# Four modulation vectors moved into attention and onto VectorE, a fourth projection bank, and S5 operators on VectorE

## Chip, cores, metric

The kernel runs on one core of one Trainium2 chip. The metric is the device time of one execution in microseconds (us). Three executions of the kernel before took 2083.79, 2084.78 and 2093.15 us, so the median is 2084.78. The profile and the trace come from a fourth execution, which took 2093.97 us.

## What is computed

Two blocks, one after the other, on 512 tokens of width 1024, in fp32. The first block is a modulated mixer (a bidirectional state-space scan called SSD, windowed attention with 256 context keys, gates and an output projection) and a convolutional feed-forward layer. The second block joins forgetting attention, a diagonal complex state-space layer (S5) and attention to a memory. Of all this the change touches two things.

The modulation is six vectors of 1024, made from one conditioning vector:

```python
mod = jax.nn.silu(c) @ w_mod[l] + b_mod[l]
sh1, sc1, gt1, sh2, sc2, gt2 = jnp.split(mod[:, None, :], N_MOD, axis=-1)
```

Numbered 0 to 5. Vectors 0 and 1 scale and shift the mixer's input and are needed at once. Vector 2 gates the mixer's output, 3 and 4 shift and scale the feed-forward layer's input, 5 gates its output.

The S5 layer needs operators that depend on weights alone: per group of 16 channels, maps into and out of the state over blocks of eight tokens, and powers of the state's rotation over 64 blocks. They are computed on the chip, ahead of the second block.

## The kernel before

All work is in one function, `emit`, written against a tile library. The program names tiles from pools with a number of buffers; the library gives each engine its order. A planner does so when the program is built: it runs through the program in a simulation of the engines and lets each engine take, of the instructions that are ready in the simulation, the one that was written first (`high_priority` moves instructions forward, `issue_after` holds them behind another instruction of the same engine). On the chip each engine then works through its own order, and waits where an operand or a buffer isn't ready.

**Weights.** `load_w` loads 512 KB of fp32 weights into a tile `raw` (three buffers, on SP's DMA queue), copies it on ScalarE into `whi` (rounded to fp32r), and subtracts on VectorE for the low half `wlo`; both have two buffers. `dense` runs three matmuls for each of 8 blocks of 128 rows: high by high (L221), high by low (L222), low by high (L223). A full block of weights is 24 matmuls of 512 columns. The outputs are PSUM banks from `bank()`, tag "d": three of them, two during attention (`set_banks`).

**Stages in order** (us of the profiled span). Until 46: norms and modulation vectors 1 and 0. From 46 to 577, the SSD stage: for each of 16 tiles `ssd_in` projects x, B, C and z, `convs` reads the projection's bank with ScalarE and VectorE, and `ssd_heads` does the scan; `ssd_out` projects every fourth round. From 577 to 631 keys and values; from 631 to 858 attention, eight pairs of heads (`att_q`, `att`), with gates (`gate_ssd`) and, from the fifth pair on, the first half of the output projection (`half_proj` into `p2`) between. From 858 to 990 the rest of the mixer's output. From 990 to 1405 the feed-forward layer: `ffn_up(0)`, `ffn_down(0)`, `ffn_up(1)`, `ffn_down(1)`. Then the second block.

**Modulation vectors.** `mod_steps` makes one vector in eight steps. Each step has a `raw` tile with 128 rows of the vector's 1024 columns and runs four matmuls over 256 columns each, with 32 columns of weights (`csil`, whose first two columns hold the silu of the conditioning); they add up in one PSUM bank, in its four groups of 32 partitions. After the last step ScalarE copies the bank, two transposes bring it into column form, and VectorE adds the bias into `modx`. Vectors 2 and 3 run with the SSD stage, two steps a round from round 5 on, in a bank of their own (`psm`, tag "m"); vector 4 runs in attention from the fifth pair on, in one of the two "d" banks; vector 5 runs in `ffn_up(0)` in a pool of two banks (`pfb`).

**S5 operators.** `s5_operators` is a generator, one piece of which is let go at fixed places of the feed-forward loops (`S5_UP`, `S5_DOWN`). Its preparation works on VectorE. Then come six rounds q: `op_maps(q)` builds `bm` and `cm` from six tensor-tensor operations of 1024 and 1152 elements per partition, on GpSimd, with scratch `x_`; `op_mm(q)` transposes and multiplies them on TensorE (its output tile uses the slot of `x_` too) and stores the results; `op_rot(q)` builds the rotations by six doublings, three operations each, on 16 to 512 elements, on GpSimd. The stores go out on GpSimd's queue (`QS`). They are read in the second block, from 1440 us on.

Of the kernel before, what the change touches and what calls it, by code (L numbers as in the profile page):

```python
# [8 lines left out]
F32 = mybir.dt.float32  # L9
# [5 lines left out]
PSUM = bass.MemoryType.PSUM  # L15
DRAM = bass.MemoryType.DRAM

P = 128
# [138 lines left out]
def emit(ctx, tc, A, out):  # L157
    nc = tc.nc

    def pool(name, bufs=1, **kw):  # L160
        return tc.tile_pool(name=name, bufs=bufs, reuse_waits="tile", **kw) if "space" not in kw else \
            tc.tile_pool(name=name, bufs=bufs, **kw)
# [46 lines left out]
    def bank(name="d"):  # L209
        return banks["p"].tile([P, 512], F32, tag="d", name=name, bufs=banks["n"])  # L210
# [122 lines left out]
            tt(modc[:, r, :].rearrange("p (j b) -> p b j", b=2), v[:, :, :, 1], bm, ADD)  # L333
        yield

    def mod_raw(r):
        def src(k):
            raw = wp.tile([P, 1024], F32, tag="raw", name="raw", bufs=3)
            DMA.dma_start(out=raw, in_=A["w_mod"][k * P:(k + 1) * P, r * 1024:(r + 1) * 1024])
            return raw  # L340
        return src

    def run(steps):
        for _ in steps:
# [98 lines left out]

    pss = ExitStack()
    ro = pss.enter_context(pool("rowsout"))
    ps = pss.enter_context(tc.tile_pool(name="pss", bufs=1, space=PSUM, reuse_waits="tile"))

    def pst(name="t"):
# [240 lines left out]
    def psm(name):  # L689
        return ps.tile([P, 512], F32, tag="m", name=name, bufs=1)  # L690

    mods = [st_ for r in (2, 3) for st_ in [mod_steps(r, mod_raw(r), 1, psm)] * 8]
    with tc.issue_after(loaded.ins), tc.issue_after(mod_end[0]):
        ssd_in(0)
    hold.clear()
# [1 line left out]
    for kt in range(16):  # L697
        if kt < 14:
            ssd_in(kt + 1)
        ssd_heads(kt)  # L700
        if kt >= 5 and kt < 13:
            for _ in range(2):
                next(mods.pop(0))
        if kt % 4 == 1 and kt > 1:
            if kt == 13:
                ssd_in(15)
            ssd_out(kt // 4 - 1)
# [193 lines left out]
    DMA.dma_start(out=s5ls, in_=A["s5p"][:, 96:144])  # L901
    att_q(0)
    first = half_proj(A["w_oa"][0], yaa, lambda m, po: act(p2[:, m], po, AF.Copy))
    mod4 = mod_steps(4, mod_raw(4))
    fill = {1: [0], 2: [1], 3: [2], 4: [3], 5: [4], 6: [5, 6], 7: [7]}
    for i in range(8):
        if i < 7:
            att_q(i + 1)
        done = att(i)
        if i == 1:  # L910
            with tc.issue_after(done.ins):
                act(s5ls, s5ls, AF.Exp)
        for m in fill.get(i, []):
            gate_ssd(m)
        if i >= 4:
            next(first)
            next(mod4)
    stt(g2, modx[:, 4, :], 1.0, col("n2g", 0, 8), ADD, MUL)
    psa.close()

# [91 lines left out]
    def s5_operators(so, pso):  # L1012
# [131 lines left out]
        def op_maps(q):  # L1144
            gs_ = slice(8 * q, 8 * q + 8)
            bc_ = so.tile([P, 4, P], F32, tag="bc_", name="bc_")
            DMA.dma_start(out=bc_, in_=A["s5p"][:, 144:].rearrange("p (a n) -> p a n", a=4)[:, :, P * q:P * q + P])

            def w4(n, k):
                return bc_[:, n].rearrange("p (g c) -> p g c", g=8).unsqueeze(2).to_broadcast([P, 8, k, 16])  # L1150
            bm = so.tile([P, 8, 8, 16], F32, tag="bm", name="bm")
            cm = so.tile([P, 8, 9, 16], F32, tag="cm", name="cm")
            x_ = so.tile([P, 8, 9, 16], F32, tag="x_", name="x_")
            tt(bm, w4(0, 8), tb1[:, gs_, ::-1].unsqueeze(3).to_broadcast([P, 8, 8, 16]), MUL, eng=G)
            tt(x_[:, :, 0:8], w4(1, 8), tb2[:, gs_, ::-1].unsqueeze(3).to_broadcast([P, 8, 8, 16]), MUL, eng=G)
            tt(bm, bm, x_[:, :, 0:8], ADD, eng=G)
            x_ = so.tile([P, 8, 9, 16], F32, tag="x_", name="x_")
            tt(cm, w4(2, 9), tc1[:, gs_].unsqueeze(3).to_broadcast([P, 8, 9, 16]), MUL, eng=G)
            tt(x_, w4(3, 9), tc2[:, gs_].unsqueeze(3).to_broadcast([P, 8, 9, 16]), MUL, eng=G)
            tt(cm, cm, x_, ADD, eng=G)  # L1160
            maps[q] = (bm, cm)
            return QS.dma_start(out=s5c2[q], in_=cm)

# [25 lines left out]
        def op_rot(q):  # L1189

            gs_ = slice(8 * q, 8 * q + 8)
            e3 = so.tile([P, 3, 8, 64], F32, tag="e3", name="e3o")
            G.memset(e3[:, 0, :, 0:1], 1.0)
            G.memset(e3[:, 1, :, 0:1], 0.0)
            x_ = so.tile([P, 2, 8, 32], F32, tag="xe", name="xe")
            for m in range(6):
                w = 1 << m
                new, xx = e3[:, 0:2, :, w:2 * w], x_[:, :, :, 0:w]
                tt(new, e3[:, 0:2, :, 0:w],
                   ec_[:, gs_, m:m + 1].unsqueeze(1).to_broadcast([P, 2, 8, w]), MUL, eng=G)  # L1200
                tt(xx, e3[:, 1::-1, :, 0:w],
                   esx[:, :, gs_, m:m + 1].to_broadcast([P, 2, 8, w]), MUL, eng=G)
                tt(new, new, xx, ADD, eng=G)
            G.tensor_copy(e3[:, 2], mg[:, gs_, 8:9].to_broadcast([P, 8, 64]))
            G.memset(e3[:, 2, :, 0:1], 0.0)
            QS.dma_start(out=s5e[:, :, gs_], in_=e3)

# [33 lines left out]
    pme.close()  # L1241
    so = ExitStack()
    spool = so.enter_context(pool("s5o", side="right"))
    pf_s = ExitStack()
    pf = pf_s.enter_context(tc.tile_pool(name="pffn", bufs=1, space=PSUM, reuse_waits="tile"))

    def pfb(name):
        return pf.tile([P, 512], F32, tag="f", name=name, bufs=2)

    mod5 = mod_steps(5, mod_raw(5), 1, pfb)  # L1250
    actf = (lambda k: hf[:, 0, k], lambda k: hf[:, 1, k])

    def conv_raw(pa, t, o):
# [8 lines left out]
        with tc.issue_after(last[0].ins), tc.issue_after(last[1].ins), tc.issue_after(ld.ins):  # L1262
            next(s5_steps, None)

    MOD_UP = (0, 1, 2, 3, 4, 5, 6, 7)
    S5_UP = (1, 2, 3, 4, 5, 6, 7, 8, 9, 12, 14, 15, 17)
    S5_DOWN = (0, 1, 4, 5, 7)

    def ffn_up(half):
        ph, pl2 = [], []  # L1270
        for j in range(11):
            t = 11 * half + j
            pa = bank("ua")
            with tc.issue_after(after[0].ins):
                dense(flat(A["w_up"][t]), KD, [actf], [pa])
            sa = ft("sa")
            conv_raw(pa, t, sa)
            act(sa, sa, AF.Silu)
            pb = bank("ub")
            dense(flat(A["w_up"][22 + t]), KD, [actf], [pb])  # L1280
            vb = ft("vb")
            conv_raw(pb, 22 + t, vb)
            tt(vb, vb, sa, MUL)
            uh = fd.tile([P, L], F32R, tag="uh", name="uh", bufs=14)
            ul = fd.tile([P, L], F32R, tag="ul", name="ul", bufs=14)
            split(uh, ul, vb)
            ph.append(uh)
            pl2.append(ul)
            if t in MOD_UP:
                next(mod5)  # L1290
            if t in S5_UP:
                s5_next()
        return (lambda k: ph[k], lambda k: pl2[k])
# [28 lines left out]
                tt(a_, a_, sq, ADD)  # L1322
    run(s5_steps)
    ps5_s.close()
    pf_s.close()
    so.close()


# [501 lines left out]
```

## Time and profile before

| | |
|---|---|
| median of three executions | 2084.78 us |
| the profiled execution | 2093.97 us |
| its span in the trace | 2092.2 us |
| mean granted clock of TensorE | 0.982 of full speed |

How to read the rows below. PE is TensorE's matmuls, PEld its weight loads, DVE VectorE, ACT ScalarE, POOL GpSimd, SP the engine that issues most loads. L221 is a line of the kernel; lines 181, 184 and 187 are helpers for an activation, a tensor-tensor and a scalar-tensor-tensor operation, so there the tile's name tells what is done. A matmul's duration holds its way through the array: matmuls overlap, and the distance of two starts is what one costs.

A row of busy time by stretch has the stretch, its length, for PE, PEld, DVE, ACT and POOL busy us with the number of instructions, then TensorE's mean granted clock, the DMA engines' share and GB/s. A row of waits names the waiting instruction, what released it, the total us, how often, and the longest. A row of a group has line, engine, operation, output<-inputs, shapes and count, then busy us, the mean ns of one, and the idle time before. A row of the timeline has start, duration, engine, line, operation and count. A row of DMA issues ends with the count, KB each, and us from issue to landing.

### The profile page before, as it was taken

How to read it: one execution, taken by the hardware profiler on the slowest of the kernel's cores; microseconds unless marked ns; L12 is line 12 of the kernel's file. 1: busy time of each engine (PE TensorE's matmuls, PEld its weight loads, DVE VectorE, ACT ScalarE, POOL GpSimd, SP SyncE). 2: the span in 40 equal slices, each digit the busy share in tenths (PEclk: the TensorE clock that was granted, in tenths of full speed). 3: DMA queues.
4: the chain of work that ended last, by engine and by line, in shares of the span. 5: the costliest groups of instructions: out<-in, count | busy, mean ns of one | idle time of the engine just before them, and what ended most of it. 6: DMA issues, size and time to landing. Idle time of an engine off the chain costs nothing.

```text
span 2092.2 us, 29510 instructions
## 1 busy us (share of the span) xinstructions
PE 1986.9 (95%) x11312; PEld 1623.7 (78%) x11312; DVE 1350.6 (65%) x2195; ACT 964.1 (46%) x1825; POOL 416.6 (20%) x539
## 2 busy tenths in 40 slices
PE   6998999998999999999999899999999899999998
PEld 4777887787788777778777677787988777888887
DVE  6878978878547775457975477664677655524444
ACT  6745555454235665334433133445465544423233
POOL 2123321212130000001054787200333100000000
PEclk9999999999999999999999999999999999999999
DMA  7443545544322023343343444436565221332332
GB/s 289 121 132 121 154 143 162 163 142 135 98 71 71 21 73 90 106 129 95 121 152 99 133 131 154 131 116 183 157 170 149 54 66 56 126 104 91 101 91 91
DMA packets 84668, 250.49 MB, mean 120 GB/s; under 512 B 11632, under 2 KB 23280, under 8 KB 83760
## 3 DMA queue, kind: packets, MB, share of 16 engines
q1 hardware_dynamic: 67376, 199.45, 30.9%
q0 software_dynamic: 17152, 49.17, 7.7%
q8 instruction: 89, 1.46, 0.3%
q14 instruction: 51, 0.42, 0.1%
HBM read 228.78 MB, written 16.65 MB: 117 GB/s over the span
## 4 chain that ended last, share of the span: by engine, by line
PE 76%; DVE 11%; issue 6%; ACT 4%; DMA 2%; POOL 1%; SPq 0%; DVEq 0%; ACTq 0%; POOLq 0%
PE p L221 6%; PE p L223 6%; PE p L222 6%; PE pl L221 4%; PE pl L223 4%; PE pl L222 4%; DVE wlo L184 3%; PE pT L807 2%; PE po L221 2%; PE pdn L223 2%; PE po L222 2%; PE po L223 2%; PE pdn L221 2%; PE ua L223 2%; PE pdn L222 2%
## 5 line engine op out<-in xcount | busy, mean ns | idle before, releaser
L184 DVE TENSOR_TENSOR wlo<-raw,whi 128x1024 fp32r<-128x1024 f32 (+3 forms) x283 | 367.3, 1299 | 341.4 <-ACT whi L181 329.5
L181 ACT ACTIVATE whi<-raw 128x1024 fp32r<-128x1024 f32 (+3 forms) x283 | 282.4, 999 | 445.0 <-PE p L222 138.4
L221 PE MATMUL pl<-hl,whi 128*128 128x512 f32 x528 | 211.7, 401 | 5.6 <-DVE cv L187 3.8
L223 PE MATMUL pl<-hl,wlo 128*128 128x512 f32 x528 | 209.7, 397 | 0.9 <-DVE wlo L184 0.7
L222 PE MATMUL pl<-hl,whi 128*128 128x512 f32 x528 | 209.8, 397 | 0.0
L223 PE MATMUL p<-h,wlo 128*128 128x512 f32 x504 | 202.0, 402 | 1.1 <-DVE wlo L184 1.1
L221 PE MATMUL p<-h,whi 128*128 128x512 f32 x504 | 201.1, 401 | 1.9 <-ACT uf L181 0.8
L222 PE MATMUL p<-h,whi 128*128 128x512 f32 x504 | 201.7, 400 | 0.0
L221 PEld LDWEIGHTS pl<-hl,whi 128*128 128x128 f32 x528 | 100.4, 190 | 25.1 <-issue 4.4
L223 PEld LDWEIGHTS pl<-hl,wlo 128*128 128x128 f32 x528 | 100.3, 190 | 22.9 <-DVE wlo L184 2.5
L221 PEld LDWEIGHTS p<-h,whi 128*128 128x128 f32 x504 | 95.5, 189 | 25.0 <-ACT uf L181 1.2
L181 ACT ACTIVATE p<-s,nm 128x512 f32<-128x512 f32 (+4 forms) x128 | 80.2, 627 | 74.4 <-PE pT L807 35.2
L223 PEld LDWEIGHTS p<-h,wlo 128*128 128x128 f32 x504 | 95.3, 189 | 23.2 <-DVE wlo L184 2.0
L782 DVE TENSOR_REDUCE nm<-s 128x1 f32<-128x512 f32 (+4 forms) x128 | 76.6, 611 | 55.7 <-PE s L1592 30.1
L222 PEld LDWEIGHTS p<-h,whi 128*128 128x128 f32 x504 | 95.3, 189 | 22.0 <-DVE h L184 0.3
L222 PEld LDWEIGHTS pl<-hl,whi 128*128 128x128 f32 x528 | 100.4, 190 | 15.2
L181 ACT ACTIVATE inj<-cs_t,dwt 128x128 f32<-128x128 f32 x256 | 81.4, 393 | 63.3 <-DVE es L635 56.0
L181 ACT ACTIVATE pt<-pT 128x512 f32<-128x512 f32 (+1 forms) x152 | 70.7, 479 | 63.1 <-PE pT L807 52.5
L640 POOL DMA_DIRECT2D cf<-rows x64 | 34.9, 552 | 298.2 <-PE y L659 292.8
L807 PE MATMUL pT<-cs_t,p 128*128 128x128 f32 x440 | 72.8, 279 | 9.9 <-ACT pt L181 9.6
L223 PE MATMUL pdn<-uh,wlo 128*128 128x512 f32 x176 | 70.9, 403 | 8.8 <-DVE wlo L184 8.8
L223 PE MATMUL ua<-hf,wlo 128*128 128x512 f32 x176 | 70.8, 402 | 8.8 <-DVE wlo L184 8.8
(543 smaller groups left out, 4955.1 us busy)
## 6 DMA issues: line engine op xcount, KB each, us to landing
raw<-in_w_ta SPq DMA_DIRECT2D x66, 512.0 KB, 3.6
raw<-in_w_tb SPq DMA_DIRECT2D x63, 512.0 KB, 3.6
raw<-in_w_up SPq DMA_DIRECT2D x44, 512.0 KB, 3.7
es<-rows POOLq DMA_DIRECT2D x64, 256.0 KB, 5.2
cf<-rows POOLq DMA_DIRECT2D x64, 256.0 KB, 4.9
raw<-in_w_mod SPq DMA_DIRECT2D x32, 512.0 KB, 3.8
raw<-in_w_os SPq DMA_DIRECT2D x16, 512.0 KB, 3.6
raw<-in_w_out SPq DMA_DIRECT2D x16, 512.0 KB, 3.8
```

Source lines behind the costliest of these rows:

```text
L181: return S.activation(o, i, f, **kw)
L184: return eng.tensor_tensor(o, a, b, op=op)
L221: T.matmul(ps, lhsT=wh, rhs=ah, start=first, stop=False)
L222: T.matmul(ps, lhsT=wh, rhs=al, start=False, stop=False)
L223: T.matmul(ps, lhsT=wl, rhs=ah, start=False, stop=last)
L640: QS.dma_start(out=c_, in_=rows[r, 1].partition_broadcast(P))
L782: V.tensor_reduce(nm[:, j:j + 1], src, axis=AX.X, op=MAX)
L807: T.transpose(pt[:, j * P:(j + 1) * P], b, ident)
```

## The change

Vectors 2 to 5 are no longer made by matmuls over 256 columns. A new `mod_sums` loads the same 32 `raw` tiles, and VectorE adds each, times its 128 conditioning values, to a scratch `acc` (the part of `p2` for tiles 6 and 7). After eight such steps TensorE sums over the partitions: eight matmuls with 128 columns of `acc` as weights and one column of ones, into a "t" bank of attention's pool; VectorE adds the bias. All 32 steps stand in attention, five behind each of the first four pairs of heads, four behind each of the next three.

The PSUM bank of tag "m" in the SSD stage goes, and the "d" banks there become four. The pool of two banks in the feed-forward stage goes too.

In `op_maps` and `op_rot` the tensor-tensor operations and the copy go from GpSimd to VectorE; the small memsets and the stores stay.

```diff
-    def mod_raw(r):
-        def src(k):
+    def mod_sums(r, step, bank, acc):
+        for k in range(KD):
             raw = wp.tile([P, 1024], F32, tag="raw", name="raw", bufs=3)
             DMA.dma_start(out=raw, in_=A["w_mod"][k * P:(k + 1) * P, r * 1024:(r + 1) * 1024])
-            return raw
-        return src
+            ck = csil[:, k, 0:1]
+            if k == 0:
+                V.tensor_scalar(acc, raw, ck, None, op0=MUL)
+            else:
+                stt(acc, raw, ck, acc, MUL, ADD)
+            if k % step == step - 1 and k < KD - 1:
+                yield
+        ps = bank("mod")
+        for j in range(8):
+            T.matmul(ps[:, j:j + 1], lhsT=acc[:, j * P:(j + 1) * P], rhs=ones[:, 0:1], start=True, stop=True)
+        tt(modx[:, r, :], ps[:, 0:8], col("bmod", r * 8, 8), ADD)
+        yield
...
     ro = pss.enter_context(pool("rowsout"))
+    set_banks(4)
...
-    mods = [st_ for r in (2, 3) for st_ in [mod_steps(r, mod_raw(r), 1, psm)] * 8]
...
-        if kt >= 5 and kt < 13:
-            for _ in range(2):
-                next(mods.pop(0))
...
-    mod4 = mod_steps(4, mod_raw(4))
+    mods = [st_ for r in (2, 3, 4, 5) for st_ in [mod_sums(r, 1, pst, p2[:, 6:8].rearrange("p k t -> p (k t)"))] * 8]
...
         if i >= 4:
             next(first)
-            next(mod4)
+        for _ in range((5, 5, 5, 5, 4, 4, 4, 0)[i]):
+            next(mods.pop(0))
...
-            tt(bm, w4(0, 8), tb1[:, gs_, ::-1].unsqueeze(3).to_broadcast([P, 8, 8, 16]), MUL, eng=G)
+            tt(bm, w4(0, 8), tb1[:, gs_, ::-1].unsqueeze(3).to_broadcast([P, 8, 8, 16]), MUL)
...
-            tt(cm, cm, x_, ADD, eng=G)
+            tt(cm, cm, x_, ADD)
...
-                tt(new, new, xx, ADD, eng=G)
-            G.tensor_copy(e3[:, 2], mg[:, gs_, 8:9].to_broadcast([P, 8, 64]))
+                tt(new, new, xx, ADD)
+            V.tensor_copy(e3[:, 2], mg[:, gs_, 8:9].to_broadcast([P, 8, 64]))
...
-    mod5 = mod_steps(5, mod_raw(5), 1, pfb)
...
-            if t in MOD_UP:
-                next(mod5)
```

The lines left out repeat the same step for the other operations of `op_maps` and `op_rot`, or take away the pool of two banks and the constant `MOD_UP`.

## Rows read from the trace of the kernel before

**Rows 1.** Part 1 of the page: busy time, share of the span, instructions.

```profile
PE 1986.9 (95%) x11312; PEld 1623.7 (78%) x11312; DVE 1350.6 (65%) x2195; ACT 964.1 (46%) x1825; POOL 416.6 (20%) x539
```

**Rows 2.** Busy time of each engine in five stretches of the span.

```profile
46.00:577.00 531.00, 501.41 (x3234) 421.64 (x3234) 421.72 (x671) 259.53 (x565) 117.35 (x162) 0.96 0.44 138
631.00:858.00 227.00, 216.48 (x1667) 173.91 (x1666) 151.01 (x332) 141.80 (x321) 7.69 (x6) 1.00 0.21 63
990.00:1124.00 134.00, 132.03 (x608) 99.21 (x608) 106.89 (x198) 57.25 (x81) 35.14 (x35) 1.00 0.40 125
1124.00:1348.00 224.00, 205.55 (x941) 163.62 (x941) 143.80 (x117) 72.21 (x101) 150.10 (x183) 0.95 0.43 134
996.00:1048.00 52.00, 51.05 (x235) 36.77 (x234) 48.16 (x129) 24.49 (x33) 0.12 (x1) 1.00 0.40 123
```

**Rows 3.** Waits of PE in the SSD stage, 46 to 577 us.

```profile
PE pc L221 <- DVE cv L187: 9.0, 2, 4.5
PE po L221 <- DVE cvc L187: 4.5, 2, 3.3
PE pl L221 <- DVE cv L187: 3.8, 1, 3.8
...
PE pc L221 <- ACT zs L181: 2.6, 1, 2.6
```

**Rows 4.** Groups of DVE instructions in the feed-forward stage, 990 to 1348 us.

```profile
L184 DVE TENSOR_TENSOR wlo<-raw,whi 128x1024 fp32r<-128x1024 f32 x51 | 91.6, 1796 | 83.1 <-ACT whi L181 79.1 <-PE o L1171 3.7
...
L184 DVE TENSOR_TENSOR ul<-vb,uh 128x512 fp32r<-128x512 f32 x22 | 29.7, 1348 | 12.6 <-ACT uh L181 12.6
...
L184 DVE TENSOR_TENSOR sm<-sm,sm 128x432 f32<-128x432 f32 x9 | 5.4, 604 | 0.0
...
L184 DVE TENSOR_TENSOR sm<-sm,sm 128x48 f32<-128x48 f32 x22 | 4.4, 208 | 0.2
```

**Rows 5.** Timeline of DVE around the longest stall, 1163 to 1181 us.

```profile
1163.08 8.58 DVE L184 TENSOR_TENSOR wlo<-raw,whi 128x1024 fp32r<-128x1024 f32 x1 [4.03 <-ACT whi L181]
...
1179.64 1.23 DVE L184 TENSOR_TENSOR wlo<-raw,whi 128x1024 fp32r<-128x1024 f32 x1 [3.84 <-ACT whi L181]
```

**Rows 6.** Timeline of POOL there: first and last of seven instructions.

```profile
1163.10 0.74 POOL L184 TENSOR_TENSOR e3o<-e3o,xe 128x256 f32<-128x256 f32 x1
...
1170.54 2.24 POOL L184 TENSOR_TENSOR e3o<-e3o,xe 128x512 f32<-128x512 f32 x1
```

**Rows 7.** Timeline of PE around one step of a modulation vector.

```profile
1088.74 0.39 PE L222 MATMUL ub<-hf,whi 128*128 128x512 f32 x1
1088.96 0.39 PE L223 MATMUL ub<-hf,wlo 128*128 128x512 f32 x1
1089.28 0.63 PE L320 MATMUL mod<-raw,csil 128*32 128x256 f32 x4
1089.84 0.50 PE L221 MATMUL ua<-hf,whi 128*128 128x512 f32 x1
```

**Rows 8.** DMA issues of the page: loads of w_mod one step long.

```profile
raw<-in_w_mod SPq DMA_DIRECT2D x32, 512.0 KB, 3.8
```

**Rows 9.** Timeline of PE where eight one-column matmuls stand.

```profile
1409.05 1.84 PE L262 MATMUL cs<-cs_t,a 128*128 128x1 f32 x16
1410.75 0.47 PE L221 MATMUL pv<-whi,hm 128*128 128x512 f32 x1
```

**Rows 10.** Groups of DVE instructions in attention, 631 to 858 us.

```profile
L797 DVE TENSOR_SCALAR p<-p,sm 128x640 f32<-128x640 f32 x32 | 17.5, 548 | 0.0
```

**Rows 11.** The chain behind the longest stall (start, us, what); six like the second follow.

```profile
1171.71 0.79 PE pdn L223
1172.51 0.43 PE pdn L221
```

**Rows 12.** Waits of POOL, 990 to 1348 us.

```profile
POOL x__10286 L184 <- DMA s5w<-w1o: 4.8, 1, 4.8
POOL x__11390 L184 <- DMA s5w<-w1o: 4.2, 1, 4.2
```

More of the change, by code (lines that the diff above doesn't have):

```diff
@@ L1153, in op_maps @@
             x_ = so.tile([P, 8, 9, 16], F32, tag="x_", name="x_")
-            tt(bm, w4(0, 8), tb1[:, gs_, ::-1].unsqueeze(3).to_broadcast([P, 8, 8, 16]), MUL, eng=G)
-            tt(x_[:, :, 0:8], w4(1, 8), tb2[:, gs_, ::-1].unsqueeze(3).to_broadcast([P, 8, 8, 16]), MUL, eng=G)
-            tt(bm, bm, x_[:, :, 0:8], ADD, eng=G)
+            tt(bm, w4(0, 8), tb1[:, gs_, ::-1].unsqueeze(3).to_broadcast([P, 8, 8, 16]), MUL)
+            tt(x_[:, :, 0:8], w4(1, 8), tb2[:, gs_, ::-1].unsqueeze(3).to_broadcast([P, 8, 8, 16]), MUL)
+            tt(bm, bm, x_[:, :, 0:8], ADD)
             x_ = so.tile([P, 8, 9, 16], F32, tag="x_", name="x_")
-            tt(cm, w4(2, 9), tc1[:, gs_].unsqueeze(3).to_broadcast([P, 8, 9, 16]), MUL, eng=G)
-            tt(x_, w4(3, 9), tc2[:, gs_].unsqueeze(3).to_broadcast([P, 8, 9, 16]), MUL, eng=G)
-            tt(cm, cm, x_, ADD, eng=G)
+            tt(cm, w4(2, 9), tc1[:, gs_].unsqueeze(3).to_broadcast([P, 8, 9, 16]), MUL)
+            tt(x_, w4(3, 9), tc2[:, gs_].unsqueeze(3).to_broadcast([P, 8, 9, 16]), MUL)
+            tt(cm, cm, x_, ADD)
             maps[q] = (bm, cm)
@@ L1199, in op_rot @@
                 tt(new, e3[:, 0:2, :, 0:w],
-                   ec_[:, gs_, m:m + 1].unsqueeze(1).to_broadcast([P, 2, 8, w]), MUL, eng=G)
+                   ec_[:, gs_, m:m + 1].unsqueeze(1).to_broadcast([P, 2, 8, w]), MUL)
                 tt(xx, e3[:, 1::-1, :, 0:w],
-                   esx[:, :, gs_, m:m + 1].to_broadcast([P, 2, 8, w]), MUL, eng=G)
-                tt(new, new, xx, ADD, eng=G)
-            G.tensor_copy(e3[:, 2], mg[:, gs_, 8:9].to_broadcast([P, 8, 64]))
+                   esx[:, :, gs_, m:m + 1].to_broadcast([P, 2, 8, w]), MUL)
+                tt(new, new, xx, ADD)
+            V.tensor_copy(e3[:, 2], mg[:, gs_, 8:9].to_broadcast([P, 8, 64]))
             G.memset(e3[:, 2, :, 0:1], 0.0)
@@ L1243, in emit @@
     spool = so.enter_context(pool("s5o", side="right"))
[L1244 to L1248, printed above, removed]
-    mod5 = mod_steps(5, mod_raw(5), 1, pfb)
     actf = (lambda k: hf[:, 0, k], lambda k: hf[:, 1, k])
@@ L1263, in s5_next @@
             next(s5_steps, None)
-    MOD_UP = (0, 1, 2, 3, 4, 5, 6, 7)
     S5_UP = (1, 2, 3, 4, 5, 6, 7, 8, 9, 12, 14, 15, 17)
@@ L1324, in emit @@
     ps5_s.close()
-    pf_s.close()
     so.close()
```

## The prediction

> **What bounds the kernel now.** First the page's part 1 [rows 1]: TensorE's matmuls cover 95% of the span, VectorE 65%, ScalarE 46%, GpSimd 20%. So whatever leaves TensorE's queue shortens the kernel, as long as nothing else is late where it leaves. Then busy time by stage [rows 2]. In the SSD stage (46 to 577 us) TensorE idles 531 - 501.4 = 29.6 us, in attention (631 to 858) 10.5, in the first part of the feed-forward stage 2.0 and in its second part (1124 to 1348) 224 - 205.55 = 18.45, there with a mean granted clock of 0.95. Two of these have one kind of cause. In the SSD stage the waits of a projection's first matmul are for the convolution or the silu that still reads a projection bank [rows 3]: these four make 19.9 us. In the second part of the feed-forward stage the wait is for the low half of the weights (wlo) on VectorE, and that subtraction is itself stretched: 51 of them take 1.796 us in the mean [rows 4], against 1.23 us where GpSimd rests, the last of [rows 5]. The worst lasts 8.58 us [rows 5], and through it GpSimd runs S5 work, seven instructions one after the other from 1163.10 to 1172.78 [rows 6].
>
> **The vectors' matmuls go.** One step of a modulation vector on TensorE stands between the matmuls at 1088.96 and 1089.84 [rows 7]: 0.88 us where the spacing is otherwise 0.22 (1088.74 to 1088.96), so it costs 0.66. There are 32 steps, one per load [rows 8]: 21.1 us, 10.6 in the SSD stage, 5.3 in attention, 5.3 in the feed-forward stage. The transposes and the copy behind each vector are left out. In their place come four times eight matmuls of one column with 128 weight columns. The same form stands at 1409.05, sixteen records for eight matmuls, and the next matmul begins 1.70 us later [rows 9]: 4 x 1.7 = 6.8 us, all in attention. Net -14.3 us; attention's TensorE work grows by 1.5. The Trainium skill (TensorE: Matmul & The Clock Gate, "Wait — 56ns, not 53.3ns?") gives a start-to-start floor of about 25 ns however few the columns; by that the 64 records would cost an estimated 1.6 us and the forecast would fall by 5. The row has 0.106 us per record, the weight loads included, so the row is taken.
>
> **The vectors on VectorE, in attention.** 28 multiply-adds over 128x1024 have two SBUF inputs as wlo has: 28 x 1.23 = 34.4 us. The four that begin a vector have one tensor; a tensor-scalar of 640 takes 0.548 us [rows 10], so between that and 1.23, say 0.9: 3.6 us. Together 38 us. Attention's VectorE load goes from 151 to 189 of 227 us [rows 2], 67% to 83%. The queue is in order: behind each multiply-add stand the softmax's maxima and scalings and the next wlo; each waits for its load, 3.8 us from issue to landing [rows 8], and for the sum before it. On SP's queue 24 more 512 KB loads come into this stage, and a weight load behind one waits for the same three raw slots; so far such slots were held until TensorE came to the step, now VectorE frees them. Bounds: nothing, if all 38 us fall into the 76 us in which VectorE rests, up to 38, if each holds up the softmax and through it TensorE. TensorE's idle time there is 10.5 us at 67%; I take half of that again, +5, since the rows are nearer to hidden than to exposed. The sums' scratch is the part of p2 that the half projection's last pair of tiles fills, so a late last vector would hold one of the two projection banks; that is in the upper bound. The bank that the fifth vector held through the second half of attention comes free; its gain is taken as nothing.
>
> **The fourth bank in the SSD stage.** The trace has no run with four. Bounds: nothing, if the convolutions simply stay late (VectorE is busy 421.7 of 531 us there), and the 19.9 us of [rows 3]. A bank more lets one further projection (24 x 0.22 = 5.3 us) run before the oldest bank must be drained, longer than the longest of these waits, 4.5. But VectorE at 79% will set the next wait. I take half, -10.
>
> **The S5 maps and rotations move.** On VectorE a tensor-tensor costs 0.158 us + 1.03 ns per element, from 48 and 432 elements [rows 4]. Six rounds of three operations on 1024 and three on 1152: 18 x 1.21 + 18 x 1.35 = 46 us. Six rounds of 18 rotations of 16 to 512 elements (3024 in all): 6 x (18 x 0.158 + 3.1) = 36; six copies of at most 0.69: 4. Together 86 us. Against that the stretching goes: wlo 51 x (1.796 - 1.23) = 29, ul 22 x (1.348 - 0.69) = 14.5 [rows 4]. VectorE then has 250.7 + 86 - 43 = 293 us of work in stages that shrink from 358 to about 330: 89%. What TensorE gets back: the 18.45 us of idle time, and the half speed behind it. After the 8.58 us stall the matmuls go at 0.43 us to 1175.49 [rows 11], the 1.2 GHz level, against 0.22; about 2 us each for the three such stalls, 6 in all. So up to -24.5. What is late next: VectorE itself. Three map operations that do not depend on each other (3.8 us) can stand ahead of a wlo that has some 3 us to spare (5.3 less 1.23 and the like on ScalarE): 0.8 x 5. And the maps' scratch slot waits for a DMA, 4.8 and 4.2 us [rows 12]; on GpSimd nobody stood behind, on VectorE a wlo does: 9.0 less twice 3 makes 3. I take +7, bounds 0 and the rival below. The S5 stores and small memsets stay on GpSimd's queue, where they wait for VectorE instead; only the second half of the kernel reads them. Net -17.5.
>
> **Sum.** -14.3 + 5 - 10 - 17.5 = -36.8 us. The profiled execution took 2093.97 us, 9.2 above the median of the runs shown, 2084.78; taken from the median, 2048.
>
> **Rivals.** (a) Attention becomes VectorE's: the multiply-adds hold up the softmax at their full length. For it: 83% load, an in-order queue, waits for loads inside it. Against it: 38 us of rest remain, and each blocks for 1.23 us only. Then +38 instead of +5: 2081, no change. (b) Slower: the planner puts a whole S5 round (6 map operations and 19 others, 86 / 6 = 14.3 us) in front of a wlo in the feed-forward stage, in the five rounds that wait for an earlier round's matmuls and so come late. TensorE then idles 14.3 - 3 = 11.3 and gets 2 us of half speed, 13.3 x 5 = 66 instead of 7: +59, so 2107. It decides from (36.8 + 7) / 5 = 8.8 us per round on. Against it: from 996 to 1048 VectorE already runs S5's preparation between the wlo, busy 48.16 of 52 us, and TensorE loses one, the last of [rows 2]. The Trainium skill (Perfetto Trace Analysis, "Optimizing Scalar/DVE Operations") says that with VectorE saturated, moving work to GpSimd may make sense; that speaks for this rival, and [rows 4, 5] against it as long as the two collide. (c) The change does not do what it says: the fourth bank leaves the waits where they are, and VectorE's own S5 work takes all that the collisions cost. Left is -14.3 + 5: 2075.
>
> **Numbers.** A difference of 0.5%, 10.4 us, is about what a measurement of this kernel can tell from none. Forecast (all terms about as sized, or better) 0.68; (a) 0.12; (b) 0.10; (c) 0.10, on the border, half to either side. Faster 0.73, same 0.17, slower 0.10. Low end: all four bank waits gone, no new waits on VectorE: -14.3 - 19.9 - 24.5 = -58.7, and the 2 us of the first feed-forward part and some half speed in the SSD stage, 2020. High end: (a) with some waits beside it, 2086; above it lies (b).
>
> **What would show it.** Right: no one-step modulation matmuls in the SSD and feed-forward stages; wlo near 1.23 us throughout the feed-forward stage and TensorE's idle time there under 10 us; the waits of [rows 3] halved; VectorE at some 190 us in attention with TensorE idling 15. Wrong: wlo short but late, behind S5 operations; TensorE idle for more than 25 us in attention; the convolution waits unchanged.

## The result and the profile after

The kernel after took 2063.38 us (median of four, 2062.18 to 2066.59), the kernel before 2084.28 (four, three of them those known before the prediction, 2080.72 to 2093.15). The ratio is 0.9894, 95% interval 0.9866 to 0.9922: faster by 20.9 us, where 36.8 were forecast. The profiled execution of after took 2063.76 us; it lies 30.2 us below the one of before, which was the longest of the first executions of that kernel. In 39 executions run later beside the experiments, on three chips, the kernel before took 2081.17 to 2098.54 us, with a median of 2091.83; so the four executions of this comparison lie on its short side, and 20.9 us may be too little. The kernel after wasn't run again there. Later comparisons are therefore made as ratios to runs of the kernel before on the same chip, and the stages below from the profiled executions.

Part 1 of the page, answering [rows 1]:

```profile
PE 1964.2 (95%) x11112; PEld 1622.0 (79%) x11112; DVE 1395.9 (68%) x2377; ACT 962.2 (47%) x1821; POOL 263.8 (13%) x389
```

TensorE is busy for 22.7 us less, VectorE for 45 more, GpSimd for 153 less. Busy time by stage (stretch, length, then PE, PEld, DVE, ACT and POOL busy with counts, granted clock, DMA share, GB/s), answering [rows 2]:

```profile
46.00:559.10 513.10, 483.07 (x3092) 410.62 (x3091) 418.27 (x667) 257.84 (x562) 119.25 (x163) 0.98 0.42 125
614.00:858.00 244.00, 228.01 (x1666) 186.42 (x1664) 181.24 (x365) 140.90 (x321) 9.55 (x7) 0.97 0.32 100
989.70:1116.90 127.20, 124.29 (x562) 100.55 (x562) 117.58 (x247) 59.25 (x85) 9.53 (x18) 1.00 0.36 111
1116.90:1372.80 255.90, 252.73 (x1177) 204.14 (x1176) 182.00 (x280) 100.53 (x146) 20.89 (x49) 0.99 0.43 134
```

Cut where work ends on TensorE, the first block has three stages. **A** goes from 46 us to the last matmul on `yh`, the SSD stage's output projection: 528.8 us before, 513.1 after. **B** goes from there to the first matmul on `mgh`, so it holds keys and values, attention, and the second half of the output projection: 348.4 before, 365.1 after. **C** goes from there to the last matmul of `pdn`, so it is above all the feed-forward layer: 480.0 before, 448.6 after. So A gives 15.7 us, C gives 31.4, and B takes 16.7 back. The second block is as long as before.

**A.** TensorE's waits from 46 to 559.1 us, answering [rows 3] (waiting instruction, releaser, us, times, longest):

```profile
PE pl L221 <- DVE cvc L187: 8.1, 2, 6.9
PE pl L221 <- ACT p L181: 5.1, 1, 5.1
PE po L221 <- ACT yh L181: 3.5, 1, 3.5
PE pl L221 <- ACT zs L181: 1.7, 1, 1.7
...
PE pc L221 <- DVE cv L187: 0.9, 1, 0.9
```

The two waits of 9.0 us for `cv` are one of 0.9, but other waits stand in their place, one of 6.9 us for a convolution's `cvc` among them. The 5.1 us are at the stage's start, where the first projection waits for a bank that an activation is still reading. TensorE idles 30.0 of 513.1 us, no less than the 29.6 of [rows 2].

**C.** The groups of VectorE from 990 to 1348 us, answering [rows 4]:

```profile
L184 DVE TENSOR_TENSOR wlo<-raw,whi 128x1024 fp32r<-128x1024 f32 x55 | 67.3, 1223 | 45.4 <-ACT whi L181 45.1
...
L184 DVE TENSOR_TENSOR ul<-vb,uh 128x512 fp32r<-128x512 f32 x22 | 15.1, 688 | 7.0 <-ACT uh L181 7.0
```

The weights' subtraction takes 1.223 us in the mean and at most 1.23, the other 0.688: neither is stretched any more. TensorE idles 6.1 us in the two stretches of C's feed-forward part, at a granted clock of 0.99 to 1.00.

**B.** Here the loss begins with one sum. VectorE, from two stretches of its timeline: the eighth and last multiply-add of vector 2, then the multiplication that begins vector 3:

```profile
617.07 1.27 DVE L187 SCALAR_TENSOR_TENSOR p<-raw,csil,p 128x1024 f32<-128x1024 f32 x1
...
675.00 0.74 DVE L344 TENSOR_SCALAR p<-raw,csil 128x1024 f32<-128x1024 f32 x1
```

57 us lie between them. Vector 3 uses the same scratch, so its first step may not overwrite it before TensorE's one-column matmuls have read it, and these stand late in TensorE's order. TensorE's timeline there:

```profile
672.98 1.90 PE L351 MATMUL mod<-cs_t,p 128*128 128x1 f32 x16
...
689.99 0.50 PE L221 MATMUL pl<-hl,whi 128*128 128x512 f32 x1 [3.02 <-ACT whi L181]
```

Meanwhile loads for vector 3 hold all three `raw` slots. SP's queue, its timeline around the gap and its longest waits:

```profile
631.09 0.33 SPq L341 DMA_DIRECT2D raw<-in_w_mod  x1
...
675.77 7.01 SPq L341 DMA_DIRECT2D raw<-in_w_mod  x4
...
684.37 1.72 SPq L215 DMA_DIRECT2D raw<-in_w_ta  x2
...
SPq L341 <- DVE sm L804: 47.1, 3, 44.3
SPq L341 <- DVE p L344: 31.0, 2, 29.2
```

Between 631.4 and 675.8 us the queue issues nothing (the wait of 44.3 us; the row names `sm`, the instruction right behind vector 3's first step), and the next weight load (`in_w_ta`) comes at 684.37, behind four more of `in_w_mod`. So TensorE has no projection to put between two softmaxes until 690. In steps of 10 us:

```profile
640.00:650.00 10.00, 7.43 (x72) 5.73 (x71) 7.95 (x19) 8.07 (x21) 1.28 (x1) 1.00 0.01 2
650.00:660.00 10.00, 9.72 (x84) 8.22 (x83) 7.82 (x21) 6.81 (x17) 0.00 (x0) 0.83 0.00 1
660.00:670.00 10.00, 7.67 (x69) 5.52 (x68) 6.41 (x18) 7.25 (x19) 0.00 (x0) 1.00 0.01 2
670.00:680.00 10.00, 9.64 (x84) 8.92 (x84) 9.20 (x21) 5.24 (x15) 0.00 (x0) 0.83 0.27 79
680.00:690.00 10.00, 6.21 (x65) 4.72 (x63) 8.99 (x17) 5.40 (x13) 0.00 (x0) 1.00 0.77 247
```

It idles for 9.3 of these 50 us (in the version below with neither loads nor sums for 1.0), and 20 of them have a granted clock of 0.83, that is, a third of the time at the 1.2 GHz level; each time a stretch with over 2 us of idle time went before. Vector 4 waits in the same way (its first step at 724.11), and TensorE idles for 3.2 us from 710 to 740 and has a granted clock of 0.66 from 720 to 730. Vector 5 waits too (772.68), but that costs nothing that the trace shows: from 740 to 840 us TensorE is busy for 99.96 of 100 us at full clock. From the end of A to the last matmul on `y` in attention, 282.3 us became 298.8: idle time 13.8 to 19.3, busy time 268.5 to 279.5. Of these 11.0 us of busy time some 2.3 are work (four times 1.90 less the 5.3 of vector 4's old matmuls); most of the other 8.7 is half speed: one stretch of 10 us with a granted clock of 0.66 and two with 0.83 are 6.8 us of clock lost.

### The profile page after: what moved, and what is told of

Its sections match the earlier page's. It is cut to its first block, busy times and chain, and to the rows that moved or that the text cites. A ratio compares the mean times of both kernels' runs of the same rounds, so it can differ in the third digit from the quotient of the medians.

```text
span 2062.0 us, 29154 instructions
## 1 busy us (share of the span) xinstructions
PE 1964.2 (95%) x11112; PEld 1622.0 (79%) x11112; DVE 1395.9 (68%) x2377; ACT 962.2 (47%) x1821; POOL 263.8 (13%) x389
## 4 chain that ended last, share of the span: by engine, by line
PE 69%; DVE 11%; issue 8%; ACT 3%; DMA 3%; POOL 2%; DVEq 0%; ACTq 0%; POOLq 0%; SPq 0%
PE p L221 6%; PE p L223 6%; PE p L222 6%; PE pl L223 3%; PE pl L221 3%; PE pl L222 3%; PE pT L816 2%; PE ua L223 2%; PE pdn L221 2%; PE pdn L223 2%; PE pdn L222 2%; PE po L223 2%; PE ub L223 2%; PE ub L222 2%; PE ub L221 2%
## 5 line engine op out<-in xcount | busy, mean ns | idle before, releaser
L184 DVE TENSOR_TENSOR wlo<-raw,whi 128x1024 fp32r<-128x1024 f32 (+3 forms) x283 | 330.1, 1167 | 256.3 <-ACT whi L181 254.4
L181 ACT ACTIVATE whi<-raw 128x1024 fp32r<-128x1024 f32 (+3 forms) x283 | 282.3, 999 | 473.5 <-PE p L222 139.4
```

Of the source, the lines that this page charges most:

```text
L181: return S.activation(o, i, f, **kw)
```

## The experiments

The table gives the stages of their profiled executions, cut as above, the median of their times (us), and its ratio to the kernel before on the same chip. The ratio of the kernel after rests on the four executions above; those of the experiments rest on 8 to 11 executions of the kernel before, with medians of 2090 to 2092 us. Every edit is planned anew, and the engines' orders can differ beyond it: the first one-column matmuls stand at 672.98 us in the kernel after and at 686.47 with neither loads nor sums.

| kernel | A | B | C | us | ratio, 95% interval |
|---|---|---|---|---|---|
| before | 528.8 | 348.4 | 480.0 | 2084.28 | 1 |
| after | 513.1 | 365.1 | 448.6 | 2063.38 | 0.9894 (0.9866 to 0.9922) |
| S5 part alone | 530.2 | 348.4 | 455.4 | 2071.35 | 0.9902 (0.9885 to 0.9918) |
| all but the S5 part | 509.3 | 369.0 | 457.4 | 2076.96 | 0.9932 (0.9915 to 0.995) |
| three banks | 523.9 | 370.4 | 447.6 | 2081.21 | 0.995 (0.993 to 0.9969) |
| own slots | 512.7 | 375.4 | 446.5 | 2070.71 | 0.9897 (0.988 to 0.9915) |
| no loads | 512.4 | 366.5 | 446.9 | 2063.37 | 0.9881 (0.9852 to 0.9909) |
| narrow sums | 511.9 | 368.2 | 441.2 | 2059.62 | 0.9869 (0.9837 to 0.99) |
| other queue | 513.6 | 378.9 | 443.2 | 2071.26 | 0.991 (0.9881 to 0.9938) |
| other queue, own slots | 510.5 | 367.3 | 449.0 | 2064.45 | 0.9886 (0.9857 to 0.9915) |
| neither loads nor sums | 514.7 | 347.3 | 445.0 | 2046.10 | 0.9785 (0.9761 to 0.981) |
| three vectors later | 513.6 | 367.0 | 452.0 | 2068.94 | 0.989 (0.9867 to 0.9912) |
| the same, first bank passed over | 511.7 | 364.9 | 452.4 | 2067.21 | 0.989 (0.9868 to 0.9912) |
| spread | 512.5 | 356.8 | 454.9 | 2059.73 | 0.9847 (0.9823 to 0.9871) |

**The S5 part alone.** The kernel before with only this edit, repeated for the other operations of the two functions:

```diff
-            tt(bm, bm, x_[:, :, 0:8], ADD, eng=G)
+            tt(bm, bm, x_[:, :, 0:8], ADD)
...
-            G.tensor_copy(e3[:, 2], mg[:, gs_, 8:9].to_broadcast([P, 8, 64]))
+            V.tensor_copy(e3[:, 2], mg[:, gs_, 8:9].to_broadcast([P, 8, 64]))
```

> The kernel before with the S5 maps and rotations alone moved to VectorE; the vectors and the banks stay. If the collision with GpSimd on SBUF made the stalls of the feed-forward stage, wlo is near 1.23 us there, TensorE idles under 8 us in it (before 20.5) and the time falls by 22 to 30 us, to 2055 to 2062. If the stalls came from the planner's order instead, VectorE's added 86 us keep wlo late and the time stays within 10 us of before.

C fell by 24.6 us, A and B stayed within 1.4. The median fell by 20.7 us, a little short of the 22 expected at least. In its feed-forward stage `wlo` takes 1.223 us in the mean of 59, against 1.719 in the kernel before. There, in the kernel before, TensorE waited for it like this (988.2 to 1403 us):

```profile
PE ua L223 <- DVE wlo L184: 8.8, 4, 6.8
PE pdn L223 <- DVE wlo L184: 8.8, 3, 7.0
```

In this kernel the waits (990 to 1380 us) are down to these, and TensorE idles for 3.8 us:

```profile
PE pdn L223 <- DVE wlo L184: 1.7, 2, 0.8
PE ua L223 <- DVE wlo L184: 1.6, 2, 1.0
PE ua L222 <- DVE hf L184: 0.3, 1, 0.3
```

So the collision of VectorE and GpSimd cost what [rows 4 to 6] made of it, and the price of VectorE's own S5 work is next to nothing.

**All but the S5 part.** The kernel after with `eng=G` put back.

```diff
-            tt(bm, bm, x_[:, :, 0:8], ADD)
+            tt(bm, bm, x_[:, :, 0:8], ADD, eng=G)
```

> The changed kernel with the S5 operations back on GpSimd: vectors in attention, four banks. The two traces give the SSD stage -16 us, attention +17.5, and vector 5 out of the feed-forward stage -5.3: about -4, so 2076 to 2084. If the vectors' move were worth the -14.3 + 5 - 10 = -19 us of the forecast, 2062 to 2068, and the S5 part would have to be worth next to nothing.

C fell by 22.6 us, where the 5.3 of the fifth vector's matmuls were expected, although the collision is still there (`wlo` 1.623 in the mean, the longest 5.06 instead of 8.58). Taken one by one the two parts give 24.6 and 22.6 us in C, together only 31.4: 15.8 us are the same us. TensorE's busy time in C's feed-forward part fell from 394.6 to 380.2 us, of which the steps' matmuls are 5.3; most of the other 9.1 is half speed that went, as the granted clock's mean rose from 0.975 to 0.991. Why the stalls are shorter without the modulation loads there wasn't taken further.

**Three banks.**

```diff
-    set_banks(4)
```

> The changed kernel with three projection banks in the SSD stage instead of four (the fourth stays unused). If the fourth bank is worth the forecast's 10 us, 2073. If it only trades the waits of the convolutions for a late start (its first projection begins at 54.5 us, against 45.8 before), 2058 to 2066, with the first projection back near 46 us.

A is 10.8 us longer than in the kernel after, so the fourth bank is worth that. Against the kernel before, A is only 4.9 us shorter, though 16 steps of 0.66 us are gone from TensorE. Where the rest went stands in this kernel's waits of TensorE in A:

```profile
PE pc L221 <- DVE cv L187: 9.5, 2, 5.0
PE pl L221 <- DVE cv L187: 6.4, 2, 3.8
PE po L221 <- DVE cvc L187: 3.6, 2, 2.2
PE po L221 <- ACT yh L181: 3.5, 1, 3.5
```

With three banks TensorE reaches the convolutions earlier and waits for them; 3.8 us in the second row were a single wait in [rows 3], here there are two, and the last row was 0.3 before. The late start comes with the fourth bank: the first projection begins at 46.77 us here, at 54.49 in the kernel after, whose A is the shorter all the same.

**Own slots.** 24 of the 32 loads go to two parts of `p2`, not into `raw`.

```diff
-            raw = wp.tile([P, 1024], F32, tag="raw", name="raw", bufs=3)
+            raw = own.pop(0) if own else wp.tile([P, 1024], F32, tag="raw", name="raw", bufs=3)
...
+    own = [p2[:, m:m + 2].rearrange("p k t -> p (k t)") for m in (2, 4)] * 12
```

> The changed kernel with two load buffers of their own for the vectors' first 24 loads (parts of p2 that are still free), so that these loads no longer take the three weight buffers. If attention lost its 17.5 us to weights that come late behind the vectors' loads, no wait of the weight copy for a load is left before the sixth pair of heads, and the time falls by 6 to 14 us, to 2049 to 2057. If it lost them to VectorE's 38 us, the time stays within 4 us of 2063.

B grew by 10.3 us. The sums still come late here (the first at 693.85 us, the second vector's first step at 695.82), and then SP's queue issues 13 loads of `w_mod` over 59 us ahead of any weight. This kernel loses time earlier too: from 578 to 598 us TensorE idles for 7.8 us at a granted clock of 0.66, in the kernel after for 2.6 at full clock. So B's growth is not that of the slots alone.

**No loads, and narrow sums.** The first leaves out the loads of `w_mod`, so vectors 2 to 5 are made of other data:

```diff
-            raw = wp.tile([P, 1024], F32, tag="raw", name="raw", bufs=3)
-            DMA.dma_start(out=raw, in_=A["w_mod"][k * P:(k + 1) * P, r * 1024:(r + 1) * 1024])
+            raw = f(hl[:, 0, 0:2].rearrange("p k t -> p (k t)"))
```

> The kernel after, but the 32 multiply-adds read two tiles of the mixer's normalised input that already stand in SBUF; the 32 loads of w_mod are left out, so vectors 2 to 5 hold other values. VectorE's work and order stay as large. From the end of the SSD stage to the first matmul of the output projection (mgh) the kernel before takes 348 us and the kernel after 365. Queue theory: the 17 us are lost because five modulation loads stand in a row on SP's queue, wait for raw slots, and the two weight loads behind them come late, so TensorE has no projections to put between the softmax's waits, idles, and is granted half speed. Then this kernel takes 345 to 352 us there and the whole ratio is near 0.981. Rival, VectorE's load: the multiply-adds themselves hold up the softmax; then the stage keeps 360 to 366 us and the ratio stays near 0.989.

The second keeps the loads and leaves out most of the sums:

```diff
-                stt(acc, raw, ck, acc, MUL, ADD)
+                stt(acc[:, 0:64], raw[:, 0:64], ck, acc[:, 0:64], MUL, ADD)
```

> The kernel after with all 32 loads, but the 28 multiply-adds work on 64 of the 1024 columns, so the vectors' sums over the other columns are left out; some 1.1 us less on VectorE each, 31 us in all. Rival, VectorE's load: the stage from the SSD stage's end to the output projection falls from 365 to about 350 us, the ratio to about 0.982. Queue theory: the loads stand in the queue as before, so the stage keeps 358 to 365 us and the ratio stays within 0.003 of 0.989.

By the conditions set for them the first speaks against the queue theory, the second against the theory of VectorE's load: B stays at 366.5 and 368.2 us. Without loads the second vector still waits for the first one's sums, at 690.2 us, and then eight of its steps come in a row, with the softmax's instructions between them. TensorE and VectorE (first and third of the five busy times) in that kernel:

```profile
685.00:695.00 10.00, 10.00 (x93) 8.76 (x91) 7.86 (x16) 5.56 (x15) 0.00 (x0) 1.00 0.19 52
695.00:705.00 10.00, 7.49 (x73) 5.78 (x71) 9.96 (x17) 5.50 (x13) 0.00 (x0) 1.00 0.01 2
705.00:715.00 10.00, 6.69 (x35) 5.10 (x35) 9.35 (x19) 5.30 (x13) 1.27 (x1) 0.83 0.00 0
```

Here VectorE is nearly full and TensorE idles 5.8 of the last 20 us. This kernel loses time in a second place too: with no load to wait for, five multiply-adds run in a row at 564 us, and from 575 to 595 TensorE idles 7.0 us and runs at a granted clock of 0.83, so that the loads' own share is not settled by it. With the loads and almost no work (narrow sums) the slots are locked as before (SP's queue takes 46.6 us over five loads from 630.84 on).

**Another queue, and another queue with own slots.** In the first one word changes; the second adds the slots in `p2` for all 32 loads and 7, 7, 6, 6, 6 steps behind the first five pairs.

```diff
-            DMA.dma_start(out=raw, in_=A["w_mod"][k * P:(k + 1) * P, r * 1024:(r + 1) * 1024])
+            QS.dma_start(out=raw, in_=A["w_mod"][k * P:(k + 1) * P, r * 1024:(r + 1) * 1024])
```

> The kernel after, but the 32 loads of w_mod are issued on GpSimd's queue instead of SP's; they keep the three raw slots. If the order in SP's queue alone costs the 17 us: stage 348 to 353 us, ratio near 0.981. If the slots cost them as well (a weight load that takes the slot of a modulation load still waits for its multiply-add): stage 355 to 365 us, ratio 0.985 to 0.990. If neither, as VectorE's load would have it: 365 us. A new cost is possible: the rope's operations on GpSimd stand behind a load that waits for its slot, and a late query holds up the scores.

> The loads of w_mod on GpSimd's queue and all 32 into two slots of their own (parts of p2 that the half projection fills later), with the 32 steps behind the first five pairs of heads (7, 7, 6, 6, 6). No weight load waits for a modulation load any more, in queue or slot. Queue and slot theory: stage near 350 us, ratio near 0.982, below both e4 (0.990) and e7. VectorE's load: the multiply-adds are now denser in the first five pairs, so the stage stays at 365 us or more.

Neither gained: 378.9 and 367.3 us in B. In the second no weight waits for a modulation load, yet vector 3 begins at 690.18 us, after sums at 688.21. From 700 to 740 us, behind this, TensorE idles for 8.9 us at granted clocks of 0.64 to 0.84, where with neither loads nor sums it idles for 3.4 at full clock. So the late sums are followed by a loss without any help of queue or slot. Why the first of the two kernels lost still more wasn't taken further. The second also lost time to a new collision. VectorE and GpSimd, from their timelines:

```profile
566.91 10.24 DVE L187 SCALAR_TENSOR_TENSOR p<-p,csil 128x1024 f32<-128x1024 f32 x2 [3.03 <-DMA p<-in_w_mod]
...
564.73 10.01 POOL L184 TENSOR_TENSOR p<-p,rby 128x512 f32<-128x512 f32 x8
```

The first of the two multiply-adds took 8.92 us instead of 1.28 while GpSimd ran through the rest of eight instructions, one after the other, of which it met the second; TensorE then idled 4.1 us from 575 to 585, at a granted clock of 0.83.

**Neither loads nor sums.** Both left out together; only the one-column matmuls and the bias stay, on other data.

```diff
-        for k in range(KD):
...
-                stt(acc, raw, ck, acc, MUL, ADD)
...
+        acc = f(hl[:, 0, 0:2].rearrange("p k t -> p (k t)"))
+        for k in range(KD - 1):
+            yield
```

> The kernel after without the 32 loads of w_mod and without the 32 multiply-adds; only the four times eight one-column matmuls and the bias stay, on other data, so vectors 2 to 5 hold other values. From the end of the SSD stage to the first matmul on mgh: 365 us in the kernel after, 366.5 without the loads, 368 with narrow sums, 348 before. If loads and multiply-adds are each enough to make the stage late (two causes, one behind the other): 340 to 350 us here, ratio near 0.978. Rival: neither matters, and the stage is long for another reason (the order that the planner gives attention with no modulation matmuls in it, the half-speed stretches): 360 us or more, ratio near 0.988.

B is 347.3 us. Loads and sums together cost 17.8 us in B, and either of them alone as much (19.2 without the loads, their second place included, and 20.9 with narrow sums). Attention from the end of A to the last `y`, in this kernel:

```profile
560.70:841.60 280.90, 269.32 (x1986) 225.30 (x1984) 178.32 (x369) 162.78 (x351) 26.00 (x18) 1.00 0.17 50
```

**Three vectors later.** Vector 2 stays in attention (8 steps over six pairs); 4, 3 and 5 stand beside the second half of the output projection and the matmuls on `mgh`, loaded on GpSimd's queue into parts of `p2`, with a scratch of their own.

```diff
-        for _ in range((5, 5, 5, 5, 4, 4, 4, 0)[i]):
+        for _ in range((2, 2, 1, 1, 1, 1, 0, 0)[i]):
...
+    for n, _ in zip((2, 4, 5, 5), half_proj(A["w_oa"][1], yab, att_half)):
+        for _ in range(n):
+            next(mods.pop(0))
```

> The kernel after with only vector 2 in attention (8 steps over six pairs of heads); vectors 4 and 3 beside the second half of the output projection and vector 5 beside the matmuls on mgh, loaded on GpSimd's queue into parts of p2 that are read out. There TensorE is busy for 66.2 of 66.2 us and VectorE for 33. If VectorE's work and the loads cost only where TensorE waits for the softmax: end of SSD to mgh falls from 365 to about 350 us, mgh to the end of the down projections stays at 449, ratio near 0.982. Rival: 24 multiply-adds on VectorE delay wlo there as they delayed the softmax: mgh comes as late as in the kernel after, ratio 0.988 or above.

Attention is as short as with nothing in it (281.1 us to the last `y`, against 280.9): one vector there, with no second that waits for its sums, costs nothing. The gain was lost behind it. TensorE's waits from 858 to 925 us, and the stretches around them:

```profile
PE mod L351 <- DVE macc L187: 8.0, 1, 8.0
...
888.00:898.00 10.00, 2.76 (x13) 1.95 (x11) 7.08 (x9) 2.17 (x3) 1.17 (x3) 0.87 0.64 211
898.00:908.00 10.00, 9.23 (x34) 8.09 (x35) 5.43 (x8) 0.63 (x1) 2.16 (x4) 0.62 0.63 211
```

This time the one-column matmuls stand too early in TensorE's order: the whole engine waits 8.0 us for VectorE's last step, and then runs at half speed for a while.

**The first bank passed over.** The same with one more line, so that the first projections don't meet the bank that is still read.

```diff
     set_banks(4)
+    bank("skip")
```

> The same with one more line: the first of the four banks is passed over once, so that the first projections of the SSD stage don't begin in the bank that an activation still reads (in the kernel after the first projection starts at 54.5 us instead of 45.8, after 5.1 us of waiting for it). If that start is lost for good: SSD's end 2 to 5 us earlier than in f2, ratio 0.001 to 0.0025 lower. Rival: the scan's first round sets the pace there, not the projections: no difference.

No difference that can be told: the ratio is the same, A is 1.9 us shorter, and the wait of 5.1 us for that activation is still among TensorE's waits. The edit didn't do what it was meant to, so that start stays open.

**Spread.** Two vectors in attention, one beside the output projection, one beside `mgh`; each vector's one-column matmuls one step after its last multiply-add. The two later ones are loaded on GpSimd's queue and have a scratch of their own, as above.

```diff
-            if k % step == step - 1 and k < KD - 1:
+            if k % step == step - 1:
...
-        for _ in range((5, 5, 5, 5, 4, 4, 4, 0)[i]):
+        for _ in range((3, 3, 3, 3, 2, 2, 2, 0)[i]):
```

> The kernel after with the 32 multiply-adds spread thinner: vectors 2 and 4 in attention (18 steps, three or two behind a pair), vector 3 beside the second half of the output projection, vector 5 beside the matmuls on mgh, and each vector's one-column matmuls one step later than its last multiply-add. In f2, 8 steps in attention cost nothing (its last matmul on y at 840.7 us, as with none) and all was lost again in one place, where TensorE's queue stood 8.0 us before the one-column matmuls and then ran at half speed. If it is the number of steps per stretch that costs, and a sum that stands too early in TensorE's queue: last matmul on y near 845, mgh at 910 to 915, ratio 0.979 to 0.983. Rival: any queue that carries the steps pays for them in full; then 16 steps cost attention 8 to 9 us and the later ones as much again, ratio 0.987 or above.

At 0.9847 it is the lowest time of a version that computes everything; its interval still touches that of the kernel after. The one place in attention where a vector waits for another's sums shows again: the last step of vector 2, the sums on TensorE, the first step of vector 4.

```profile
627.82 1.27 DVE L187 SCALAR_TENSOR_TENSOR p<-raw,csil,p 128x1024 f32<-128x1024 f32 x1
...
698.48 1.90 PE L351 MATMUL mod<-cs_t,p 128*128 128x1 f32 x16
...
700.50 0.74 DVE L344 TENSOR_SCALAR p<-raw,csil 128x1024 f32<-128x1024 f32 x1
```

Here too SP's queue stands still in between, for 60 us:

```profile
631.10 10.17 SPq L341 DMA_DIRECT2D raw<-in_w_mod  x3
701.27 1.65 SPq L215 DMA_DIRECT2D raw<-in_w_ta  x2
```

To the last `y` it took 290.4 us, 9.5 more than with nothing there. From 924 to 990 us it lost further time at a granted clock of 0.90 (0.97 in the kernel after), so C is 6.3 us longer than in the kernel after.

**What the runs leave open.** To the last `y` it took 280.9 us with no steps, 281.1 with one vector, 290.4 with two, 298.8 with four. One vector has no wait for an earlier sum, two have one, four have three, of which the last cost nothing. That fits the scratch, and the order of events shows the wait in every trace that lost time in attention; no run takes away the wait alone, so that it is the cause is argued and not shown. It would also fit a price per step that starts above eight. A second scratch, or the sums placed earlier in TensorE's order, tells these apart and wasn't tried.

## Why the prediction was right, and where its sizes were off

The sign was right and 2063 lies in the range, but 20.9 us are little more than half of the 36.8. By stages the forecast was A -20.6, B +6.5, C -22.8 and came to -36.9; the profiled executions give -15.7, +16.7 and -31.4, in sum -30.4. The runs' medians lie only 20.9 apart, since the kernel before varies by more than ten us between executions and its profiled one was long. That the stages' sum lies as near to the forecast as it does is in part luck: A gave 4.9 us less and B lost 10.2 more than forecast, and C gave 8.6 more.

**The vectors' matmuls go (-14.3).** Their price per step was read off correctly, but in A it was not all on the path: removing 10.6 us of work shortened A by 4.9 (three banks). TensorE then reached the convolutions' banks earlier and waited there. The one-column matmuls took 1.84 to 2.56 us for sixteen records, as [rows 9] had it. The estimate that the prediction made from the Trainium skill (TensorE: Matmul & The Clock Gate, "Wait — 56ns, not 53.3ns?"), 1.6 us for 64 records and so 0.4 for sixteen, is far from that: its floor is not what sets the pace of this form.

**The vectors on VectorE (+5): the term that failed.** With the 1.5 us of work it should have been 6.5 and measured 16.7. To the last `y`, where 16.5 of these fall, idle time grew by 5.5 us and TensorE's work by some 2.3; the other 8.7 are for the most part half speed, which the sum put at nothing in attention. So the +5 of idle time came out, and the sign given for it too (16.0 us from 614 to 858, where 15 were forecast), but by luck: it was not sized from what made it. The size of VectorE's work was right: 36.3 us for 28 multiply-adds, 4.1 for the four others, against 34.4 and 3.6. What the step missed is a wait, by the order of events in the traces, and half speed behind it. It counted, of one vector, that each step waits for the sum before it, and it saw that the loads hold `raw` slots. But it took these slots to come free at VectorE's pace. Between two vectors the one scratch passes through TensorE, whose order has the first sums 55 us later; the slots and SP's queue pass the wait on to the weights (44.3 us), and TensorE idles and falls to half speed behind it. That loads and sums together cost the 17.8 us of B is shown; that they do so by this wait is read from the traces, and the price per step isn't ruled out. The prediction's "half of 10.5" had no row behind it for such a chain; the rows that it weighed were shares of busy time.

**The fourth bank (-10).** 10.8 measured (after against three banks). Against three banks TensorE idles 6.2 us less in A (30.0 instead of 36.2) and is busy for 4.6 less, at a granted clock of 0.98 instead of 0.97. Against the kernel before the idle time is the same: the forecast that the waits of [rows 3] would be halved holds for waits of their kind (10.7 us instead of 19.9, or 11.1 instead of 23.0 with the small ones), but others took their place, the start's 5.1 us among them. That the new bank would meet an older tile at the start wasn't seen.

**The S5 part (-17.5).** Alone it gave 24.6 in C, the whole of its upper bound, so the +7 for new waits behind VectorE was too cautious: no `wlo` was late by more than 2.0 us. VectorE was busy for 299.6 of 383.1 us in the feed-forward stage, 78%, not 89%. In the same stage the fifth vector's steps weighed more than their 5.3 us of matmuls (22.6 by themselves, with their loads and the pool of banks gone too), but the two gains overlap by 15.8.

**The rivals.** (a) falls as put: it wasn't the multiply-adds' length that cost (narrow sums change nothing), but attention did lose nearly half of the 38 us, by another way. (b) falls: VectorE's S5 rounds never held up a `wlo` for long, the longest `wlo` wait of TensorE in C being 2.0 us. (c) falls with the bank's 10.8 us and the S5 part's 24.6.

## What to carry to other kernels

When a sum moves from an engine to another, follow its buffer through every engine that touches it: a single scratch that a second engine has to read before the next sum may begin ties both queues' orders together, and whatever waits in the same slots and queue waits along. Two gains that both shorten the same waits don't add: cost them against the stage with the other already made. And a small matmul placed into a full queue is dangerous at both ends, too late for the one who needs its buffer, too early for the engine that has to wait for its input.

## What was not expected of the hardware

An instruction of VectorE with two SBUF inputs was held not for one instruction of GpSimd but through a row of them. In [rows 5, 6] `wlo` ends at 1171.66 us, so its usual 1.23 us begin at 1170.43, just before the sixth of the seven instructions ends. The seventh then takes 2.24 us, where the same operation takes 1.27 to 1.30 in the five other rounds. In the version with another queue and own slots the multiply-add begins at 566.91 us, in the second of eight instructions of 1.27 to 1.30 each, and ends at 575.83; its usual 1.28 us begin at 574.55, just before the eighth ends. It isn't always so. At 1074 us in the kernel before, VectorE had its turn behind the one instruction that ran, and the next one of GpSimd was held in turn (VectorE's row, then GpSimd's):

```profile
1074.02 2.10 DVE L184 TENSOR_TENSOR wlo<-raw,whi 128x1024 fp32r<-128x1024 f32 x1
...
1073.63 1.41 POOL L184 TENSOR_TENSOR e3o<-e3o,sm 128x512 f32<-128x512 f32 x1
1075.00 2.06 POOL L184 TENSOR_TENSOR xe<-e3o,sm 128x512 f32<-128x512 f32 x1
...
1168.44 2.13 POOL L184 TENSOR_TENSOR x__10528<-bc__10520,sm 128x1152 f32<-128x1152 f32 x1
```

The last row is the sixth of the seven in the first long stall. The Trainium skill (SBUF — State Buffer, "SBUF: two separate sides") says that of two such instructions the one that starts first gets the shared port pair for the whole instruction, and the other fully blocks. The blocking agrees, for either engine. By that rule alone VectorE might be expected to get its turn behind the one GpSimd instruction that runs, as it does at 1074 us; in the two long stalls it gets it only near the end of the row, in the first of them although its start stands 0.02 us ahead of GpSimd's. What decides between the two isn't shown.

Half speed in attention: the kernel before ran there at full clock from end to end, though it too had stretches of 10 us with 8.16 and 7.76 us of TensorE work (from 710 and 730 us on); the kernel after fell to 0.83 behind stretches of 7.43 and 7.67, and to 0.66 behind one of 8.80 (from 710 us on). About half of what attention lost is this: 8.7 of the 16.5 us to the last `y`, by the busy time that is not work, or 6.8 by the granted clock.
